# Token tile 0 taken four groups ahead at the ends and heads of layers, and a feed order for each kind of unit

## The chip, the cores and the metric
One core of one Trainium2 chip runs the whole kernel. The metric is the device time of one execution in microseconds; the kernel before is given by the median of 3 runs. Engines: PE is TensorE (matrix products), PEld its weight load, DVE VectorE, ACT ScalarE, POOL GpSimd, SP the engine whose queue issues most DMAs. "L172" is line 172 of the kernel before.

## The reference, cut to what matters
Two layers over 256 tokens of width 2048, batch 1, all in fp32. Each layer is a mixer and a feed-forward net (FFN), each followed by a residual addition and a LayerNorm. The mixer of layer 0 (here mixer 0) is a gated MLP beside a pooling; that of layer 1 (mixer 1) is a gated linear recurrence over 16 heads.

```python
for l in range(2):
    if l % 2 == 0:
        h = x @ ev_w_in[e]                              # 2048 x 3072
        ...
        mix = concatenate([ya, yb]) @ ev_w_out[e]       # 2048 x 2048
    else:
        q, f_logit, inp, g = split(x @ od_w_in[o], 4)   # 2048 x 8192
        y = rms_norm(hgrn2(q, f_logit, inp, lb_all[l]), od_norm_g[o])
        mix = (y * sigmoid(g)) @ od_w_out[o]            # 2048 x 2048
    x = layer_norm(ALPHA * x + mix, ln1_g[l], ln1_b[l])
    x = layer_norm(ALPHA * x + conv_ffn(x, ...), ln2_g[l], ln2_b[l])

def conv_ffn(x, w_up, conv_w, conv_b, w_down):
    h = x @ w_up                                        # 2048 x 11264
    ...                                                 # causal convolution of width 3
    a, v = split(hc, 2)
    return (silu(a) * v) @ w_down                       # 5632 x 2048
```

## The kernel before
**Tiles.** The 256 tokens are two token tiles, t = 0 and 1, of 128 (`x_t[t]`). Weights come as tiles of 512 inputs by 512 outputs, 1 MB each. An fp32 product is made from three products of rounded numbers: a weight w is split into a high half wh (ACT, L172) and a low half wl (DVE, L175; for the feeds in `on_pool` POOL, in four pieces), and an activation likewise; wh·xh, wl·xh and wh·xl are added up in PSUM. So one weight tile and one token tile are 12 matmuls of 512 columns: four slices of 128 inputs, three products each.

**Weights.** `Weights` is a planner that is filled before the kernel is written out: `std`, `quad` and `chain` append feeds, in the order in which the weights will be used, and loads. There are two kinds of loads. Kind 0 uses a ring of three raw tiles (`BUFS`); kind 1 uses the tiles q0 to q3 (an FFN) or qa and qb (mixer 1) of the pool `raw[1]`, one buffer each. `room` lets a load of kind 1 pass only when its phase is `open`; `W.open += 1` stands at the beginning of each FFN and of mixer 1. `take` hands out the next weight; ahead of that it issues all loads for which there is room (kind 1 first) and makes the halves of the two weights that follow. The halves lie in the pool `hl`, three buffers of wh and of wl. All loads are issued on SP's queue; in `quad` and `chain`, sums of weights are made by accumulating DMAs, which POOL issues (L77, L105).

**Layers.** `chunk` makes 512 outputs of both token tiles from four weights; with `head` it takes three weights ahead and runs them for token tile 0, then for token tile 1, then the fourth weight for both, so that token tile 0 can begin while token tile 1 of x is still being normed. After a layer's first chunk `combine` makes the sums of x for the Strassen units. `strassen` makes 2 x 2 blocks (two token tiles, two chunks) from seven products of 12 matmuls (P1 to P7), and four plain groups of 24 ("s"); "o" in its order is a place for one step of the down projection (`down`), 24 matmuls, if there is one. `UNIT_R` is the order for mixer 1, where the order of feeds made by `chain` must be the same one. In a chain P7, P6 and P4 use the tile a in turn: behind P7's cast a load is added to it for P6, behind P6's cast another for P4. Mixer 1 has four head groups `hg` of two units each; group 0 has no down steps (its first unit is two plain chunks), groups 1 and 2 have two in each unit, group 3 one.

**Later work.** Work on vectors is put off by `later(n, fn)` and called by `tick`; 12 matmuls of a unit tick 0.5. In `heads4`, `queries`, `scores`, `outputs` and `transpose_split` of a token tile follow one another in this way; `outputs(t)` makes o, and its transposes on PE make YT, the input of the down steps in the next group.

**The end of a layer.** `last_down` runs the last four down steps (c = 0 to 3) of FFN 0, mixer 1 and FFN 1; mixer 0 ends with `out_proj`. It runs c = 0 for both token tiles, then c = 1 to 3 for token tile 0, then `norm(0)`, then c = 1 to 3 for token tile 1, then `norm(1)`. `after` adds the product to x (L561) and takes statistics (L588); `norm` makes moments (L492, L485, a power on POOL L488), and then for each quarter of x two steps on DVE (L498, L499) and `transpose_split`: four transposes on PE (L480) into a PSUM tile of the tag aux, and its high and low halves on ACT (L270) and DVE (L271). The tag aux has four buffers, the banks acc another four; the products of token tile 1, c = 1 to 3, go to aux:

```python
        def out_bank(t, c):
            if t == 0 or c == 0:
                b = banks.pop(0)
                banks.append(b)
                return acc.tile([P, 512], F32, name="ps", tag=b)
            return aux.tile([P, 512], F32, name="pd", tag="aux")
```

The framework puts the instructions of each engine in a fixed order before run time, by its own estimate of when each is ready, and by the order of the code where several are.

## Time and profile before

| | us |
|---|---|
| median of 3 runs | 2228.1 (2226.89 to 2231.41) |
| the profiled execution | 2226.97 |
| its span in the trace | 2225.3 |
| PE busy | 2164.7 (97%) |
| DVE busy | 1769.9 (80%) |
| ACT busy | 1234.0 (55%) |
| POOL busy | 128.9 (6%) |
| mean granted clock of PE | 0.988 of full |

Busy time of PE includes moments in which matmuls run at the lower clock, and an engine's share is a mean over stages. What PE waits for, and how many matmuls it gets through in a stretch, are read from the views below.

### The profile page before, as it was taken

The page shows a single profiled execution, that of the slowest core. Times are in us where ns is not written, and L with a number is a line of the kernel's source. Part 1 is how long each engine was busy: PE and PEld are TensorE (multiplying, and loading weights), DVE is VectorE, ACT ScalarE, POOL GpSimd, SP SyncE. Part 2 cuts the span into 40 slices and gives each one's busy share as a digit, 9 for nine tenths or more (in the row PEclk, how much of TensorE's full clock was granted, in tenths as well). Part 3 has the DMA queues.
Part 4 walks back from the last instruction along what each step waited for, and adds up shares of the span by engine and source line. Part 5 has one row for each costly group of instructions (what it writes and reads, how often), then busy time and mean ns, then how long its engine had stood idle before and what let it go on. Part 6 is the DMA issues. An engine that isn't in the chain of part 4 may idle for free. (4 is left out here: it accounts for less than half of the span.)

```text
span 2225.3 us, 24817 instructions
## 1 busy us (share of the span) xinstructions
PE 2164.7 (97%) x9887; PEld 1787.4 (80%) x9887; DVE 1769.9 (80%) x1706; ACT 1234.0 (55%) x1153; POOL 128.9 (6%) x140
## 2 busy tenths in 40 slices
PE   9999999999999999979999999989999999999997
PEld 7888788888888888868788888768888888888885
DVE  5545888888888888877677877778888888888888
ACT  5443365555555555536475757536556555555552
POOL 1000200000000000020000101030000000000000
PEclk9999999999999999989999999999999999999999
DMA  8647456767767667546788687755677666777742
GB/s 320 265 160 287 147 184 222 241 228 245 231 219 221 219 226 241 194 146 204 208 246 256 218 257 225 226 185 178 232 241 233 224 221 215 224 243 248 243 153 114
DMA packets 71795, 489.00 MB, mean 220 GB/s; under 512 B 8464, under 2 KB 9120, under 8 KB 13952
## 3 DMA queue, kind: packets, MB, share of 16 engines
q1 hardware_dynamic: 60656, 411.56, 49.6%
q0 software_dynamic: 11024, 75.86, 17.0%
q8 instruction: 77, 1.26, 0.2%
q14 instruction: 38, 0.31, 0.0%
HBM read 443.34 MB, written 2.11 MB: 200 GB/s over the span
## 5 line engine op out<-in xcount | busy, mean ns | idle before, releaser
L175 DVE TENSOR_TENSOR wl<-w,wh 128x2048 fp32r<-128x2048 f32 (+1 forms) x471 | 1051.8, 2236 | 346.8 <-ACT wh L172 345.1
L172 ACT ACTIVATE wh<-w 128x2048 fp32r<-128x2048 f32 (+1 forms) x495 | 894.7, 1813 | 637.2 <-PE pd L553 271.1
L399 PE MATMUL ps<-wh,xh 128*128 128x512 f32 x1188 | 470.4, 396 | 5.2 <-ACT wh L172 5.2
L399 PE MATMUL ps<-wl,xh 128*128 128x512 f32 x1188 | 464.7, 391 | 3.4 <-DVE wl L175 3.4
L399 PE MATMUL ps<-wh,xl 128*128 128x512 f32 x1188 | 464.2, 391 | 0.0
L553 PE MATMUL pd<-wh,yh 128*128 128x512 f32 x760 | 296.9, 391 | 0.0
L553 PE MATMUL pd<-wl,yh 128*128 128x512 f32 x760 | 296.2, 390 | 0.0
L553 PE MATMUL pd<-wh,yl 128*128 128x512 f32 x760 | 295.9, 390 | 0.0
L399 PEld LDWEIGHTS ps<-wh,xh 128*128 128x128 f32 x1188 | 224.1, 189 | 51.4 <-ACT wh L172 6.5
L399 PEld LDWEIGHTS ps<-wl,xh 128*128 128x128 f32 x1188 | 224.3, 189 | 49.5 <-DVE wl L175 5.0
L399 PEld LDWEIGHTS ps<-wh,xl 128*128 128x128 f32 x1188 | 224.0, 189 | 47.2
L399 PE MATMUL ps<-wh,sh 128*128 128x512 f32 x432 | 168.7, 390 | 1.2 <-ACT u L411 1.2
L399 PE MATMUL ps<-wl,sh 128*128 128x512 f32 x432 | 168.2, 389 | 0.0
L399 PE MATMUL ps<-wh,sl 128*128 128x512 f32 x432 | 168.1, 389 | 0.0
L553 PEld LDWEIGHTS pd<-wh,yl 128*128 128x128 f32 x760 | 142.9, 188 | 30.1 <-DVE yl L271 0.4
L553 PEld LDWEIGHTS pd<-wh,yh 128*128 128x128 f32 x760 | 143.1, 188 | 29.6
L553 PEld LDWEIGHTS pd<-wl,yh 128*128 128x128 f32 x760 | 143.0, 188 | 29.6
L332 PE MATMUL ps<-wl,xh 128*128 128x512 f32 x384 | 152.5, 398 | 2.4 <-POOL wl L175 2.3
L332 PE MATMUL ps<-wh,xh 128*128 128x512 f32 x384 | 153.1, 400 | 1.6 <-ACT wh L172 1.6
L332 PE MATMUL ps<-wh,xl 128*128 128x512 f32 x384 | 151.2, 394 | 0.0
L771 DVE SCALAR_TENSOR_TENSOR hc<-ph,cw,hc 128x254 f32<-128x254 f32 (+1 forms) x352 | 145.6, 475 | 1.0 <-ACT hc L768 1.0
L768 ACT ACTIVATE hc<-ph,cw 128x256 f32<-128x256 f32 x176 | 89.3, 557 | 64.9 <-DVE hc L771 61.3
(227 smaller groups left out, 2181.5 us busy)
## 6 DMA issues: line engine op xcount, KB each, us to landing
w<-in_w_up SPq DMA_DIRECT2D x176, 1024.0 KB, 4.9
w<-in_w_down SPq DMA_DIRECT2D x88, 1024.0 KB, 4.9
w<-in_w_od_in SPq DMA_DIRECT2D x64, 1024.0 KB, 6.3
w<-w POOLq DMA_DIRECT2D x40, 1024.0 KB, 8.0
w<-in_w_od_in POOLq DMA_DIRECT2D x21, 1024.0 KB, 9.0
w<-in_w_ev_in SPq DMA_DIRECT2D x20, 1024.0 KB, 5.6
w<-in_w_ev_out SPq DMA_DIRECT2D x16, 1024.0 KB, 4.8
w<-in_w_od_out SPq DMA_DIRECT2D x16, 1024.0 KB, 6.4
```

Of the source, the lines that this page charges most:

```text
L172: self.nc.scalar.activation(h[:, sl], w[:, sl], AF.Copy)
L175: eng.tensor_tensor(out=l[:, sl], in0=w[:, sl], in1=h[:, sl].bitcast(F32), op=ALU.subtract)
L332: T.matmul(ps[t], s[:, k, ts], m[:, k], start=(gi == 0 and k == 0 and i == 0), stop=(gi == n - 1 and k == 3 and i == 2))
L399: T.matmul(bank_, x[:, k, ts], m[:, k], start=(id(bank_) not in started), stop=(k == 3 and i == 2), skip_group_check=True)
L553: T.matmul(ps, x[:, k, t * P:(t + 1) * P], m[:, k], start=(k == 0 and i == 0), stop=(k == 3 and i == 2))
L768: A.activation(ob, pt[:, k], AF.Identity, scale=cw[:, 2, blk:blk + 1], bias=cw[:, 3, blk:blk + 1])
L771: V.scalar_tensor_tensor(out=ob[:, s:S], in0=pt[:, k, 0:S - s], scalar=cw[:, w, blk:blk + 1], in1=ob[:, s:S], op0=ALU.mult, op1=ALU.add)
```

## The change
Five things change.
1. `last_down` gives all products the banks acc. It runs the last `n_skew` groups (4 in the FFNs, 3 in mixer 1) for token tile 0, then the same for token tile 1. The norm of token tile 0 is cut into quarters, one behind each product of token tile 1 (with `n_skew=3` two behind the first).
2. `chunk` with `head` runs all four groups for token tile 0, then all four for token tile 1, and calls `after(t)` right behind each. It no longer ticks.
3. The fourth weight that is then held needs halves beyond the three buffers of `hl`. `extra` puts them into two quad tiles: the fourth feed of each FFN and of mixer 1, and the first feed of the last down steps of each FFN. To leave those tiles free, `W.open += 1` moves behind the first chunk of a layer, and so do the quad loads.
4. `UNIT_R` becomes three orders, by the number of down steps in the unit (0, 1 or 2; the last is the order before).
5. `outputs(t)` comes 1 tick (0.5 in group 3) behind the later of `scores(t)` and `after_i(t)`, where it came 1 + t ticks (half of it in group 3) behind `after_i`; the transposes of o come 1.5 ticks behind the outputs, where it was 1 (0.5 in group 3 as before).

```diff
--- before.py
+++ after.py
@@ -25,7 +25,9 @@
 ALPHA = float(np.float32(4.0 ** 0.25))
 WIN = (2, 4, 8, 16)
 SKEW = 3
-UNIT_R = ("P1", "s", "P7", "s", "P3", "P2", "P6", "o", "P5", "o", "P4", "s", "s")
+UNIT_R = (("P1", "P7", "s", "P3", "s", "P6", "P2", "P5", "s", "P4", "s"),
+          ("P1", "s", "P7", "s", "P3", "P2", "P6", "o", "P5", "s", "P4", "s"),
+          ("P1", "s", "P7", "s", "P3", "P2", "P6", "o", "P5", "o", "P4", "s", "s"))
 UNIT = ("P1", "s", "P2", "s", "P3", "o", "P7", "o", "P6", "o", "P5", "o", "P4", "s", "s")
 BUFS = 3
 EDGE = 244
@@ -46,6 +48,8 @@
         self.ring = {}
         self.done = {}
         self.on_pool = set()
+
+        self.extra = {}
 
 
     def _load(self, ap, tag):
@@ -99,6 +103,7 @@
 
         nc = self.nc
         a, b = self._load(aps[3], "qa"), self._load(aps[2], "qb")
+        unit = UNIT_R[len(others)]
         rest, others = iter(rest), iter(others)
 
         def add(ap):
@@ -112,7 +117,7 @@
         products = {"P7": (a, (), None, lambda: add(aps[0])), "P3": (b,), "P6": (a, (b,), None, t1),
                     "P5": (b,), "P4": (a,)}
         plain = {"P1": aps[0], "P2": aps[1]}
-        for f in UNIT_R:
+        for f in unit:
             if f in products:
                 self._feed(*products[f])
             else:
@@ -157,8 +162,9 @@
     def cast(self, pieces=1, between=None):
         i = self.n_cast
         w = self.feeds[i]["r"]["tile"]
-        h = self.hl.tile([P, 4, 512], F32R, name=f"wh{i}", tag="wh")
-        l = self.hl.tile([P, 4, 512], F32R, name=f"wl{i}", tag="wl")
+        pool, tags = (self.raw[1], self.extra[i]) if i in self.extra else (self.hl, ("wh", "wl"))
+        h = pool.tile([P, 4, 512], F32R, name=f"wh{i}", tag=tags[0])
+        l = pool.tile([P, 4, 512], F32R, name=f"wl{i}", tag=tags[1])
         if i in self.on_pool:
             pieces, eng = 4, self.nc.gpsimd
         else:
@@ -219,6 +225,7 @@
 
     def plan_ffn(l):
         W.on_pool |= {len(W.feeds) + i for i in range(2)}
+        W.extra[len(W.feeds) + 3] = ("q1", "q3")
         up, down = a["w_up"][l], a["w_down"][l]
         W.phase += 1
         for p in range(11):
@@ -230,10 +237,12 @@
             W.quad([up[p, 0], up[p, 1], up[11 + p, 1], up[11 + p, 0]],
                    [up[p, 2], up[p, 3], up[11 + p, 2], up[11 + p, 3]], now)
         W.std([down[c, 9] for c in (2, 3)])
+        W.extra[len(W.feeds)] = ("q1", "q3")
         W.std([down[c, 10] for c in range(4)])
 
     plan_ffn(0)
     W.on_pool |= {len(W.feeds) + i for i in range(2)}
+    W.extra[len(W.feeds) + 3] = ("qa", "qb")
     W.phase += 1
     wi, wo = a["w_od_in"], a["w_od_out"]
     for hg in range(4):
@@ -334,12 +343,16 @@
                              stop=(gi == n - 1 and k == 3 and i == 2))
 
         order = list(range(n))
-        first = order[:SKEW] if head else []
+        first = order if head else []
         last = order[-SKEW:] if tail else []
         ws = [W.take() for _ in first]
         for t in range(2):
             for gi, w in zip(first, ws):
                 mm(gi, w, t)
+            if first:
+                after(t, ps[t])
+        if first:
+            return
         for gi in order[len(first):n - len(last)]:
             if gi == n - 1:
                 tick(9)
@@ -570,47 +583,53 @@
             tick(0.5)
             add_x(t, c, ps, scale)
 
-    def last_down(get, g_ap, b_ap, final):
+    def last_down(get, g_ap, b_ap, final, n_skew=4):
 
         gt, bt = load_gb(g_ap, b_ap)
         sts = [small.tile([P, 4, 6], F32, name=f"st{t}") for t in range(2)]
         new = [new_T("x", g) for g in range(4)] if not final else None
-        pool_of = {}
-
-        def out_bank(t, c):
-            if t == 0 or c == 0:
-                b = banks.pop(0)
-                banks.append(b)
-                return acc.tile([P, 512], F32, name="ps", tag=b)
-            return aux.tile([P, 512], F32, name="pd", tag="aux")
+        def out_bank():
+            b = banks.pop(0)
+            banks.append(b)
+            return acc.tile([P, 512], F32, name="ps", tag=b)
 
         def after(t, c, ps):
             V.bn_stats(sts[t][:, c], add_x(t, c, ps, False))
 
-        def norm(t):
-            mean, rs = moments(sts[t])
-            for q in range(4):
-                qs = slice(q * 512, (q + 1) * 512)
-                normalize(x_t[t][:, qs], x_t[t][:, qs], mean, rs, gt[:, qs], bt[:, qs])
-                if final:
-                    nc.sync.dma_start(out[t * P:(t + 1) * P, qs], x_t[t][:, qs])
-                else:
-                    transpose_split(new[q], x_t[t][:, qs], t)
+        def norm(t, q, mean, rs):
+            qs = slice(q * 512, (q + 1) * 512)
+            normalize(x_t[t][:, qs], x_t[t][:, qs], mean, rs, gt[:, qs], bt[:, qs])
+            if final:
+                nc.sync.dma_start(out[t * P:(t + 1) * P, qs], x_t[t][:, qs])
+            else:
+                transpose_split(new[q], x_t[t][:, qs], t)
 
         tick(9)
         Ts = get()
-        w = W.take()
-        for t in range(2):
-            ps = out_bank(t, 0)
-            product(ps, w, Ts, t)
-            after(t, 0, ps)
-        ws = [W.take() for _ in range(3)]
-        for t in range(2):
-            for c, w in zip((1, 2, 3), ws):
-                ps = out_bank(t, c)
+        for c in range(4 - n_skew):
+            w = W.take()
+            for t in range(2):
+                ps = out_bank()
                 product(ps, w, Ts, t)
                 after(t, c, ps)
-            norm(t)
+        skewed = range(4 - n_skew, 4)
+        ws = [W.take() for _ in skewed]
+        for c, w in zip(skewed, ws):
+            ps = out_bank()
+            product(ps, w, Ts, 0)
+            after(0, c, ps)
+        mean, rs = moments(sts[0])
+        todo = list(range(4))
+        for c, w in zip(skewed, ws):
+            ps = out_bank()
+            product(ps, w, Ts, 1)
+
+            while len(todo) > 3 - c:
+                norm(0, todo.pop(0), mean, rs)
+            after(1, c, ps)
+        mean, rs = moments(sts[1])
+        for q in range(4):
+            norm(1, q, mean, rs)
         return new
 
 
@@ -739,7 +758,6 @@
         with ExitStack() as pools:
             wk = pools.enter_context(tc.tile_pool(name=f"workf{l}", bufs=1))
             raw[1] = pools.enter_context(tc.tile_pool(name=f"rawq{l}", bufs=1))
-            W.open += 1
             cwp = pools.enter_context(tc.tile_pool(name=f"cw{l}", bufs=1))
             cw = cwp.tile([P, 4, 2 * NF], F32, name="cw")
             G.dma_start(cw, a["conv"][l].rearrange("p (j n) -> p j n", j=4))
@@ -793,6 +811,7 @@
             done = ready(0)
             chunk(XT, 4, conv(0, done), head=True)
             tmp = [wk.tile([P, 4, S], F32, name="cmb", tag="hc", bufs=2) for _ in range(2)]
+            W.open += 1
             XS = combine(XT, *(v[:, :, ts] for v in tmp for ts in (np.s_[0:P], np.s_[P:S])))
             chunk(XT, 4, conv(1, done))
             for p in range(1, 11):
@@ -811,7 +830,6 @@
         yp = pools.enter_context(tc.tile_pool(name="ymix1", bufs=1))
         raw[1] = pools.enter_context(tc.tile_pool(name="rawq", bufs=1))
         wk = pools.enter_context(tc.tile_pool(name="work1", bufs=1))
-        W.open += 1
         YT = []
         tri_r = wk.tile([P, P], F32R, name="tri_r")
         A.activation(tri_r, tri, AF.Copy)
@@ -843,6 +861,7 @@
         def heads4(hg):
             qs = slice(hg * 512, (hg + 1) * 512)
             eb, kd, ke, kx, qd, qx, vv, o_s, st, gg = {}, {}, {}, {}, {}, {}, {}, {}, {}, {}
+            parts = [0, 0]
 
             def tile_f(name="f"):
                 return wk.tile([P, 512], F32, name=name, tag="ta", bufs=2)
@@ -927,12 +946,19 @@
                 for k in range(4):
                     T.matmul(px[:, k], kx[t][:, k], qd[t][:, k, hi], start=True, stop=True)
                 A.activation(att[t][lo, :, hi], px, AF.Copy)
+                both(t)
 
             def after_i(t, v):
                 vv[t] = v
                 if t == 0:
                     later(0.5, state)
-                later((1 + t) / (1 if hg < 3 else 2), lambda: outputs(t))
+                both(t)
+
+            def both(t):
+
+                parts[t] += 1
+                if parts[t] == 2:
+                    later(1 if hg < 3 else 0.5, lambda: outputs(t))
 
             def state():
                 pu = aux.tile([P, 4, P], F32, name="pu", tag="aux")
@@ -968,7 +994,7 @@
                     YT.append(tuple(y))
                 if t == 1 and hg < 3:
                     bounds(hg + 1)
-                later(1 if hg < 3 else 0.5, lambda: transpose_split(YT[hg], o, t))
+                later(1.5 if hg < 3 else 0.5, lambda: transpose_split(YT[hg], o, t))
 
             def after_g(t, ps, g):
                 A.activation(g, ps, AF.Sigmoid)
@@ -984,12 +1010,13 @@
                     for t in range(2):
                         (done1, done2)[c](t, tiles[t])
 
-                strassen(XT, XS[0], tile_of, done, downs, UNIT_R)
+                strassen(XT, XS[0], tile_of, done, downs, UNIT_R[len(downs)])
 
             n_out = 2 if hg < 3 else 1
             downs = [lambda c=c: down(c, YT[hg - 1], hg == 1) for c in range(4)] if hg else []
             if hg == 0:
                 chunk(XT, 4, lambda t, ps: after_f(t, ps, tile_f()), head=True)
+                W.open += 1
                 tmp = [wk.tile([P, 4, P], F32, name="cmb", tag=g, bufs=2) for g in ("eb", "eb", "kd", "kd")]
                 XS.append(combine(XT, *tmp))
                 chunk(XT, 4, lambda t, ps: after_g(t, ps, tile_g()))
@@ -1003,7 +1030,7 @@
             rest = heads4(hg)
         for fn in rest:
             fn()
-        XT = last_down(lambda: YT[3], a["ln1_g"][1], a["ln1_b"][1], False)
+        XT = last_down(lambda: YT[3], a["ln1_g"][1], a["ln1_b"][1], False, n_skew=3)
         del raw[1]
 
     ffn(1, XT, True)
```

## Rows read from the trace of the kernel before

**Rows 1.** The page, section 1: busy time, share of span, instructions of each engine.

```profile
PE 2164.7 (97%) x9887; PEld 1787.4 (80%) x9887; DVE 1769.9 (80%) x1706; ACT 1234.0 (55%) x1153; POOL 128.9 (6%) x140
```

**Rows 2.** Waits of PE: who waited for whom: us in total, times, longest us.

```profile
PE pt L480 <- DVE x L499: 20.8, 8, 4.3
PE pt L480 <- DVE o L960: 5.8, 4, 1.5
PE ps L399 <- ACT wh L172: 5.2, 3, 3.8
...
PE ps L399 <- DVE wl L175: 3.4, 4, 1.8
```

**Rows 3.** PE by stretches: length, PE busy (matmuls), granted clock, DMA share, GB/s.

```profile
238.00:256.00 18.00, 13.40 (x59) 0.91 0.24 74
962.00:1000.00 38.00, 27.71 (x115) 0.82 0.43 144
1063.00:1079.00 16.00, 11.23 (x36) 0.79 0.72 238
1417.50:1427.00 9.50, 6.75 (x22) 0.82 0.80 294
1470.00:1503.00 33.00, 24.44 (x100) 0.84 0.54 166
```

**Rows 4.** The same stretches, transposes of x (tile pt) alone.

```profile
962.00:1000.00 38.00, 6.94 (x32) 0.82 0.43 144
1470.00:1503.00 33.00, 4.62 (x24) 0.84 0.54 166
```

**Rows 5.** Timeline of PE, FFN 0 to mixer 1: start, us, instruction [idle before <-releaser].

```profile
967.27 1.41 PE L480 MATMUL pt<-cst,x 128*128 128x128 f32 x8 [4.07 <-DVE x L499]
...
990.54 1.08 PE L480 MATMUL pt<-cst,x 128*128 128x128 f32 x4 [4.29 <-DVE x L499]
```

**Rows 6.** Timeline of PE, head group 0, transposes of o for token tile 1.

```profile
1116.16 0.63 PE L480 MATMUL pt<-cst,o 128*128 128x128 f32 x4 [1.44 <-DVE o L960]
```

**Rows 7.** Timelines of DVE and POOL, norm of token tile 0 (FFN 0, mixer 0).

```profile
965.06 1.41 DVE L498 SCALAR_TENSOR_TENSOR x<-x,mv,g 128x512 f32<-128x512 f32 x2
...
243.43 3.47 DVE L498 SCALAR_TENSOR_TENSOR x<-x,mv,g 128x512 f32<-128x512 f32 x2
...
241.36 12.49 POOL L175 TENSOR_TENSOR wl<-w,wh 128x512 fp32r<-128x512 f32 x8 [0.44 <-ACT wh L172]
```

**Rows 8.** Timelines of POOL, ACT and PE, mixer 1's first unit.

```profile
1059.22 0.86 POOL L105 DMA_DIRECT2D w<-in_w_od_in  x1 [15.01 <-DVE wl L175]
...
1068.27 3.71 ACT L172 ACTIVATE wh<-w 128x2048 fp32r<-128x2048 f32 x2 [4.88 <-DMA w<-in_w_od_in]
...
1070.23 0.50 PE L399 MATMUL ps<-wh,xh 128*128 128x512 f32 x1 [3.77 <-ACT wh L172]
```

**Rows 9.** Timelines of POOL and ACT, mixer 1's last unit.

```profile
1407.03 0.85 POOL L105 DMA_DIRECT2D w<-in_w_od_in  x1 [15.62 <-DVE wl L175]
...
1416.71 3.71 ACT L172 ACTIVATE wh<-w 128x2048 fp32r<-128x2048 f32 x2 [5.64 <-DMA w<-in_w_od_in]
```

**Rows 10.** Timelines of PE and DVE at the end of the kernel.

```profile
2210.71 0.39 PE L553 MATMUL pd<-wl,yh 128*128 128x512 f32 x1
...
2212.98 0.39 PE L553 MATMUL pd<-wh,yl 128*128 128x512 f32 x1
...
2212.36 1.28 DVE L561 TENSOR_TENSOR x<-x,pd 128x512 f32<-128x512 f32 x2
...
2215.46 0.69 DVE L588 BATCH_NORM_STATS2 st<-x 128x6 f32<-128x512 f32 x1
...
2220.53 1.41 DVE L499 SCALAR_TENSOR_TENSOR x<-x,rs,b 128x512 f32<-128x512 f32 x2
```

**Rows 11.** The page, section 6 (KB, us to landing); a stretch with all engines, DMA last.

```profile
w<-in_w_up SPq DMA_DIRECT2D x176, 1024.0 KB, 4.9
...
1460.00:1470.00 10.00, 10.00 (x46) 8.29 (x45) 7.73 (x8) 3.84 (x2) 0.68 (x1) 1.00 1.00 406
```

## The prediction, made before the change was run

> **What bounds the kernel now.** Read section 1 of the page first: TensorE (PE) is busy for 97% of the span, VectorE (DVE) for 80%, ScalarE (ACT) for 55%, GpSimd (POOL) for 6% [rows 1]. So the end is set by PE, and only two things can shorten the kernel: fewer PE instructions (the change removes none) or fewer moments in which PE stands still or runs slowly. Read PE's waits next. Almost all of them are of a few kinds [rows 2]: transposes of the normalized x wait for DVE (20.8 us in 8 waits), transposes of the attention output o wait for DVE (5.8 us in 4), and products in the Strassen units wait for the high and low halves of a weight (5.2 and 3.4 us).
>
> Then read PE by stretches, because a wait is only part of the loss: after one, the granted clock is low for a while. Eleven 512-column matmuls in a row start from 2210.71 to 2212.98, one each 0.227 us [rows 10]; four transposes take 0.63 us, about 0.12 us each [rows 6]. What a stretch loses is its length less 0.227 us per product matmul and 0.12 per transpose:
> - FFN 0 to mixer 1, 962 to 1000: 115 matmuls, 32 of them transposes [rows 3, 4]. 38 - 83 x 0.227 - 32 x 0.12 = **15.3 us** lost. Its two largest idle pieces are 4.07 and 4.29 us [rows 5], and the mean clock is 0.82 [rows 3], that is part of it at the lower of the two levels, 1.2 GHz.
> - Mixer 1 to FFN 1, 1470 to 1503: 100, of them 24 transposes [rows 3, 4]. 33 - 76 x 0.227 - 24 x 0.12 = **12.9 us**.
> - Mixer 0 to FFN 0, 238 to 256: 59, of them 16 transposes (token tile 0's four quarters). 18 - 43 x 0.227 - 16 x 0.12 = **6.3 us** [rows 3].
> - The first Strassen unit of mixer 1, 1063 to 1079: 36, four of them short. 16 - 32 x 0.227 - 4 x 0.12 = **8.3 us** [rows 3].
> - The last unit of mixer 1, 1417.5 to 1427: 9.5 - 22 x 0.227 = **4.5 us** [rows 3].
> - Three waits of 1.44 us and a little more for o, in head groups 0 to 2: **4.3 us** [rows 6].
>
> **The layer ends.** Before, the last products run c0 for both token tiles, then c1 to c3 for token tile 0, then its norm, then c1 to c3 for token tile 1. These last write PSUM tiles of the tag aux, whose four buffers the four transposed quarters have just taken. So no product of token tile 1 can be issued ahead of the transposes, and PE stands while DVE makes the moments and the quarters. The change gives all products the acc banks, and puts each quarter behind a product of token tile 1: 12 matmuls, 2.7 us, lie between two quarters. PE then has 36 matmuls (mixer 1) or 48 (FFN 0) beside the norm.
>
> The other end case has this shape already: at the end of mixer 0 the norm of token tile 0 runs beside 36 matmuls. It still loses 6.3 us, and the reason moves along with the change. POOL makes the low halves of the next layer's first two weights (8 pieces, 12.49 us) as soon as ACT has a free weight buffer, and during that a pair of DVE norm steps takes 3.47 us (two pairs do) where it takes 1.41 alone [rows 7]. Before, at the end of FFN 0, the norm of token tile 0 was over before POOL began. After, a buffer comes free when the second product of token tile 1 is done, so POOL begins some 5 us, two products, before the last one ends and meets the last quarters of the norm. So I don't take the loss to zero but to the measured 6.3 us: FFN 0 to mixer 1 gains 15.3 - 6.3 = **9.0 us** (bounds: 2, if all quarters are met, and 15.3). At mixer 1 there are only three products, 8.2 us, for 16 norm and split steps and three additions with statistics, so I add 1.5 us to what stays: 12.9 - 7.8 = **5.1 us** (0 to 12.9).
>
> The Trainium skill states the reason as a rule (SBUF — State Buffer, section Who interferes with whom): a DVE instruction with two inputs in SBUF and a GpSimd instruction that reads SBUF lock each other out for a whole instruction. The trace agrees: 3.47 against 1.41 us for two [rows 7]. The rule speaks against the change, which brings more such pairs together; taken for every quarter it is the first rival.
>
> **The heads.** Token tile 0 now runs all four groups (48 matmuls, 10.9 us) before token tile 1, where it ran three, so the norm of token tile 1 has 2.7 us more cover. What DVE is late by at the end of the products comes back here: eight norm steps of 0.66 us and four additions with statistics of 1.33 [rows 10] are 10.6 us, and with the splits more than the 10.9 of four products. I count nothing for that, since the head's 48 matmuls cover it. The fourth weight must be there 8.2 us into the head. Its load waits for the first weight's raw tile, which POOL holds; then it takes 4.9 us [rows 11], and its halves are two more steps on ACT and on a busy DVE. I charge **1 us** for all heads together (bounds: 1 gained, 6 lost). On ACT the two sigmoids of mixer 1's first chunk part, so the activation tables change twice more; ACT has 45% to spare [rows 1].
>
> The quad loads (four of 1 MB for each FFN, two for mixer 1, on SP's queue, with the accumulating DMA that POOL issues behind each set) wait for the head's fourth weight to be used up, as it lies in two of their buffers. They are moved past the loads of the second chunk's weights, which the head's own takes have issued, and past POOL's low halves, done by then. Their first user comes one chunk later, 96 matmuls or 21.8 us. Four MB at the 406 GB/s that the queues reached [rows 11] are 10.4 us, and an accumulating load behind takes 9 us (below). Mixer 1: 5.2 + 9 + 2 for the casts is 16 of 24.5 us (P7 now comes right behind P1). Cost nothing; if the cover is gone, the rival on the other side.
>
> **The units with few down steps.** In mixer 1's first unit POOL issues the last accumulating load of the chain at 1059.22, when P6's halves are made; ACT makes the halves of P4 at 1068.27, after 9 us, and PE, having only P5 in between, waits 3.77 us and starts P4 at 1070.23, then runs at a mean clock of 0.79 [rows 3, 8]. The unit has no down steps to fill the places marked o. The new order sets P2 and a plain group (2.7 and 5.4 us) between P6 and P4, beside P5: 8.2 us more, against a wait of 3.8. P7 to P6 gets 2.7 us more too, so the load before has no new trouble. 8.3 us go but for 0.5 that I leave: **7.8 us** (4 to 8.3). In head group 3 the same wait (issue 1407.03, halves 1416.71 [rows 9]) has a plain group more in front of it, 5.4 us against 2.8 of waits: 4.5 us. But that group no longer lies behind P4. The queries start from P4, and the outputs of head group 3 so move next to the last products, with 2.7 us less behind them. I take 2 us off: **2.5 us** (1 lost to 4.5).
>
> **The outputs.** In head groups 0 to 2 the transposes of o come 1.5 instead of 1 tick behind the outputs, half a tick being 12 matmuls or 2.7 us, and token tile 1's outputs come half a tick sooner. A wait of 1.44 us is then covered by matmuls: **4.3 us** (1 to 4.3). What waits behind is the split of y, used half a tick later at the earliest.
>
> **The tail.** PE's last matmul starts at 2212.98; DVE then is in arrears with token tile 0's norm, adds two results at 2212.36 and ends at 2221.94 [rows 10]. With token tile 0 done one product sooner DVE has 10.9 us for 5.3 of norm and 4.0 of three additions, so it waits for PE: 2213.4 + 1.4 (an addition of 0.64 and statistics of 0.69 [rows 10]) + 0.5 until the norm (now 2221.94 - 5.28 - 2216.15) + 8 x 0.66 = 2220.6, with 0.1 of gaps **1.2 us** less (0 to 1.2).
>
> **Sum.** 9.0 + 5.1 + 7.8 + 2.5 + 4.3 + 1.2 - 1.0 = 28.9 us. The profiled execution took 2226.97 us, its span 2225.3; the median of the runs is 1.1 above it. 2226.97 - 28.9 = 2198.1, so for a median **2199 us**.
>
> **The rivals.**
> 1. *POOL's low halves meet the whole norm.* Eight pieces hold up eight DVE steps by 1.0 us each ((3.47 - 1.41) / 2), 8.2 us at each of two ends, where I allow for about half. For it: in mixer 0 at least four of eight steps were met (the two pairs of 3.47 us [rows 7]); against: in FFN 0 three quarters should be over before POOL starts. 2199 + 2 x 4 = 2207.
> 2. *PE's order doesn't change where it counts*: the transposes still stand ahead of products that could cover them, as the order was fixed before run time. The ends give nothing: 2199 + 14 = 2213. Against it: the end of mixer 0, where 13 matmuls do stand between quarters.
> 3. *The units wait for bytes and not for order.* The DMA share in both stretches is 0.72 and 0.82 [rows 3], not 1. Then 7.8 and 2.5 don't come: 2209.
> 4. *All stalls go.* The ends keep 2 us each and not 6.3 and 7.8: 2199 - 10, and no charge at the heads: 2188.
> 5. *Slower: SP stands at the quad loads.* SP's queue is served in order; the first quad load waits for the head's last matmul. Were the second chunk's four weight loads placed behind it, PE would wait for 4 MB of quads (10.4 us), a load (4.9) and a cast (2) in each FFN, less what is buffered: about 16, in mixer 1 about 10. 2199 + 42 = 2241. It decides from about three of the four loads on. Against it: the code issues them first.
>
> **How the numbers follow.** Forecast 0.55, rivals 0.17, 0.07, 0.05, 0.10 and 0.06. The terms' bounds do not all meet at one end; half of them going badly costs 15 us, half going well gives 13. Range 2184 to 2216: it takes in rivals 1 to 3 and most of 4, and leaves out rival 5 and the tails, some 0.18. A measurement tells 0.2% (4.5 us) from no change: faster 0.90, within it 0.04 (rivals 2 and 3 together), slower 0.06.
>
> **What the profile after would show.** PE's waits for x fall from 20.8 us to below 10; the stretch from FFN 0 to mixer 1 loses 6 us and not 15; POOL's eight pieces lie beside DVE norm steps of 1.7 us; the wait for P4 is gone in both units; no transposes of o wait in groups 0 to 2; the new waits to look for are of products at a head on the fourth weight, and of transposes in the last products. I am wrong if the second chunk of a layer waits for loads, or if the ends lose as much as now.

## The result, and the profile after

The changed kernel took **2203.1 us** (median of four runs, 2196.8 to 2204.2) beside 2227.6 for the kernel before in the same runs: a ratio of 0.988, 95% interval 0.986 to 0.990. That is 24.5 us less, inside the predicted range and 4 us above the predicted 2199. A second set of runs gave 2199.9 (2196.0 to 2208.8), 0.986 [0.984, 0.989]. The single runs of this kernel lie up to 13 us apart; why is one of the findings below.

The profiled execution took 2203.0 us with a span of 2201.2, against 2227.0 and 2225.3 before. Section 1 of the page after, with the same columns as [rows 1]:

```profile
PE 2157.1 (98%) x9887; PEld 1779.9 (81%) x9887; DVE 1767.4 (80%) x1706; ACT 1230.3 (56%) x1150; POOL 125.8 (6%) x140
```

The same 9887 PE instructions: nothing was taken away, PE only stands or runs slowly for less time. The waits of PE after (who waited for whom: us in total, times, longest us):

```profile
PE pt L493 <- DVE x L512: 10.8, 8, 2.7
PE pt L493 <- DVE o L986: 4.2, 3, 1.4
PE pa L943 <- DVE eb L929: 3.3, 1, 3.3
PE pd L566 <- DVE x L574: 3.2, 2, 1.7
PE ps L412 <- DVE wl L181: 2.2, 3, 1.1
PE pb L485 <- DVE fl L280: 2.1, 1, 2.1
PE ps L341 <- ACT wh L178: 1.6, 2, 1.4
...
PE pt L493 <- DVE ss L500: 1.0, 1, 1.0
```

Against [rows 2]: the wait for x is halved (20.8 to 10.8); the waits of the Strassen units for a high half (5.2) are off the list; the wait for o is still there (5.8 in four, now 4.2 in three, and a fourth listed under ss); pa for eb and pd for x are new, and pb for fl has grown. In the same list before, last products waited for yh where pd now waits for x, and pb waited for 0.5 us:

```profile
PE ps L553 <- ACT yh L270: 5.0, 2, 2.5
...
PE pb L472 <- DVE fl L271: 0.5, 1, 0.5
```

PE by stretches (length, PE busy and matmuls, granted clock, DMA share, GB/s):

```profile
238.00:256.00 18.00, 13.40 (x65) 1.00 0.23 79
950.00:990.00 40.00, 35.86 (x165) 0.96 0.34 128
1063.00:1079.00 16.00, 15.30 (x84) 1.00 0.74 209
1079.00:1095.00 16.00, 13.35 (x73) 0.89 0.52 132
1376.00:1386.00 10.00, 7.39 (x30) 0.83 0.52 97
1412.00:1427.00 15.00, 15.00 (x76) 1.00 0.74 290
...
1455.00:1490.00 35.00, 32.78 (x145) 0.95 0.45 165
```

The transposes of x in two of the ends, in the same columns:

```profile
950.00:990.00 40.00, 5.42 (x32) 0.96 0.34 128
...
1455.00:1490.00 35.00, 4.76 (x28) 0.95 0.45 165
```

By the prediction's reckoning (length less 0.227 us per product matmul and 0.12 per transpose) FFN 0 to mixer 1 loses 40 - 133 x 0.227 - 32 x 0.12 = **6.0 us**, where it lost 15.3 [rows 3, 4]. From mixer 1 to FFN 1, 145 matmuls from 1455 to 1490 with 28 transposes among them lose **5.1 us**, where it was 12.9. The first unit's P4, which waited 3.77 us and left the clock at 0.79 [rows 3, 8], now comes near 1058 without a wait, and the clock from 1063 to 1079 is 1.00. But behind it, from 1079 to 1095, the clock is 0.89, and from 1376 to 1386 it is 0.83: these are the waits for eb and fl.

To compare kernels I add up, over all matmuls, the time between two starts beyond what the form takes at full clock, and call it PE's excess. The full-clock time of a form is its usual step, 0.227 us for a product matmul; taken by form or by line, it moves the totals by up to a microsecond. It is 90.8 us in the kernel before and 68.1 after: 22.7 us less. The tail from the last matmul to the end of the span fell from 12.3 to 10.9. Together 24.1, which is the difference of the two spans.

### The profile page after: what moved, and what is told of

Its sections match the earlier page's. It is cut to its first block, busy times and chain, and to the rows that moved or that the text cites. A ratio compares the mean times of both kernels' runs of the same rounds, so it can differ in the third digit from the quotient of the medians.

```text
span 2201.2 us, 24814 instructions
## 1 busy us (share of the span) xinstructions
PE 2157.1 (98%) x9887; PEld 1779.9 (81%) x9887; DVE 1767.4 (80%) x1706; ACT 1230.3 (56%) x1150; POOL 125.8 (6%) x140
## 5 line engine op out<-in xcount | busy, mean ns | idle before, releaser
L566 PE MATMUL pd<-wh,yh 128*128 128x512 f32 x736 | 287.2, 390 | 3.2 <-DVE x L574 3.2
L566 PE MATMUL pd<-wl,yh 128*128 128x512 f32 x736 | 286.5, 389 | 0.4 <-DVE wl L181 0.4
L566 PE MATMUL pd<-wh,yl 128*128 128x512 f32 x736 | 286.4, 390 | 0.5 <-DVE yl L280 0.4
L566 PEld LDWEIGHTS pd<-wh,yh 128*128 128x128 f32 x736 | 138.2, 188 | 32.5 <-DVE x L574 4.0
L566 PEld LDWEIGHTS pd<-wh,yl 128*128 128x128 f32 x736 | 138.1, 188 | 30.3 <-DVE yl L280 1.6
L566 PEld LDWEIGHTS pd<-wl,yh 128*128 128x128 f32 x736 | 138.2, 188 | 29.3 <-DVE wl L181 0.8
```

The lines of the kernel that those rows point to most:

```text
L566: T.matmul(ps, x[:, k, t * P:(t + 1) * P], m[:, k], start=(k == 0 and i == 0), stop=(k == 3 and i == 2))
```

## The experiments

Each run was timed beside the kernel before on its own chip, so ratios are compared; 0.001 of ratio is 2.2 us.

**The last products alone.** The kernel before with the new `last_down` and the two buffers for the fourth last weight, nothing else.

```
+        W.extra[len(W.feeds)] = ("q1", "q3")
         W.std([down[c, 10] for c in range(4)])
...
-    def last_down(get, g_ap, b_ap, final):
+    def last_down(get, g_ap, b_ap, final, n_skew=4):
...
```

> The kernel before with the new last products alone (all products in the acc banks, a quarter of the norm behind each product of token tile 1, and the two buffers for the fourth last weight); old heads, unit orders and outputs. Theory: these are the whole gain, 9.0, 5.1 and 1.2 us by the prediction and some 21 us as the stretches of the changed kernel show them, so 2206 to 2212 us. Rival: they need the head of four groups behind them, and without it give half: 2215 to 2220 us.

Measured 2206.3 us (2203.3 to 2208.3), 0.9895 [0.9879, 0.9910]: nearly the whole gain, as the first theory has it. Excess before and here: FFN 0 to mixer 1 (925 to 1025 us) 20.7 to 12.5, mixer 1 to FFN 1 (1425 to 1500) 16.9 to 8.8, the last products of FFN 1 (2150 to 2200) 5.9 to 2.6; the tail gives 1.4.

**The PSUM buffers alone.** The kernel before, products and norm written in the old order.

```
-            if t == 0 or c == 0:
-                b = banks.pop(0)
...
-            return aux.tile([P, 512], F32, name="pd", tag="aux")
+            b = banks.pop(0)
+            banks.append(b)
+            return acc.tile([P, 512], F32, name="ps", tag=b)
```

> The kernel before with one thing changed: all last products write PSUM tiles of the acc banks; the order in which they and the norm are written in the source stays (all of token tile 0, its norm, then token tile 1). Theory, the prediction's account: only the four aux buffers held the products of token tile 1 behind the transposes, and with other buffers they are placed ahead of them and beside them: the ends gain 10 us or more, 2207 to 2217 us. Rival: the order in the source decides, and the transposes still stand ahead of the products: 2225 to 2230 us.

Measured 2214.0 us (2213.1 to 2216.2), 0.9936 [0.9924, 0.9949]: 14 us from a change of tags. In the program built from it eight transposes of token tile 0 stand in the middle of the second of the three products of token tile 1 that used to follow them, and the next eight among the matmuls of the third, though the source still has all of them first. So the buffers were what held PE, as the prediction said. The remaining 8 to 9 us of the last products (by the medians, by the ratios) come with the new order. PE's timeline (start, us, [idle before <-releaser]) of this kernel ahead of and in FFN 0's last products:

```profile
947.90 0.50 PE L553 MATMUL ps<-wh,yh 128*128 128x512 f32 x1 [2.52 <-ACT yh L270]
969.15 0.63 PE L480 MATMUL pt<-cst,x 128*128 128x128 f32 x4 [1.06 <-DVE x L499]
975.36 0.66 PE L480 MATMUL pt<-cst,x 128*128 128x128 f32 x4 [2.61 <-DVE x L499]
```

The first line is a wait that I had not priced. It stands ahead of the last products of either FFN. With the new order it is a wait of 1.5 to 1.7 us, of a down product for x; what in the order shortens it was not taken apart.

**The heads undone.** Three groups for token tile 0, the quads opened where they were.

```
-        first = order if head else []
+        first = order[:SKEW] if head else []
...
-            if first:
-                after(t, ps[t])
-        if first:
-            return
```

> The changed kernel with heads of three groups and the old quad loads; the fourth weight's two buffers go with it. Theory, the prediction's account: the fourth group covers nothing that is short, and the head costs at most 1 us: 2201 to 2204 us. Rival: with three groups the norm of token tile 1, which still waits for POOL's low halves, is 2.7 us short of cover at each of three heads, and the clock falls behind the wait: 2208 to 2214 us, with longer waits of transposes of x.

Measured 2211.0 us (2210.1 to 2213.2), 0.9918 [0.9904, 0.9933] where the changed kernel has 0.9881 and 0.9863: the rival is right. The largest piece is at the head of FFN 1 (PE's timeline):

```profile
1475.36 1.12 PE L487 MATMUL pt<-cst,x 128*128 128x128 f32 x4 [4.37 <-DVE x L506]
```

The changed kernel has no such wait there: its longest at this end are 0.93 and 1.11 us. From 1425 to 1500 us the excess is 14.7 against 11.4, and from 1000 to 1025 it is 2.2 against 0.2; the rest of the 8 us is not placed. What the heads are worth depends on the units, as the section on the last products and the first unit shows.

**The unit orders undone.** All seven units in the old order.

```
-UNIT_R = (("P1", "P7", "s", "P3", "s", "P6", "P2", "P5", "s", "P4", "s"),
-          ("P1", "s", "P7", "s", "P3", "P2", "P6", "o", "P5", "s", "P4", "s"),
-          ("P1", "s", "P7", "s", "P3", "P2", "P6", "o", "P5", "o", "P4", "s", "s"))
+UNIT_R = (("P1", "s", "P7", "s", "P3", "P2", "P6", "o", "P5", "o", "P4", "s", "s"),) * 3
```

> The changed kernel with the old order in all seven units of mixer 1. Theory: the new orders only moved the wait of the chain, from P4 of a unit to P7 of the next unit, because P4's halves are made one plain group later and the two loads of the next unit start behind them. Then the waits of the first unit (8 us) and of the last one (5 us) come back, and the waits at 1081 us (6 us), 1380 us (5 us) and about 2 us near 1443 go: 2203 us, between 2200 and 2206. Rival, the prediction's account: the new orders are worth 7.8 and 2.5 us net, so the kernel takes 2213 us.

Measured 2204.6 us (2202.4 to 2207.5), 0.9889 [0.9873, 0.9905]: part 4, for which I had 10.3 us, is worth 2 to 5 by the medians (2203.1 and 2199.9 with it), and the intervals overlap. PE's timeline here, in the first unit and in the last:

```profile
1056.92 0.51 PE L410 MATMUL ps<-wh,xh 128*128 128x512 f32 x1 [3.72 <-ACT wh L176]
...
1406.64 0.50 PE L410 MATMUL ps<-wh,xh 128*128 128x512 f32 x1 [1.60 <-ACT wh L176]
1408.97 0.50 PE L410 MATMUL ps<-wl,xh 128*128 128x512 f32 x1 [1.82 <-DVE wl L179]
```

The old waits are back, and the new ones are gone. In the excess, in slices of 25 us: from 1050 on 7.0 and 2.6 here, 0.4 and 7.1 in the changed kernel; 1375 and 1400: 0.2 and 5.8 here, 5.0 and 0.0 there. How the wait moved is seen in the changed kernel's timelines of POOL, ACT, DVE and PE, where one unit passes into the next:

```profile
1063.53 0.84 POOL L110 DMA_DIRECT2D w<-in_w_od_in  x1 [21.12 <-DVE u L453]
...
1076.75 1.92 ACT L178 ACTIVATE wh<-w 128x2048 fp32r<-128x2048 f32 x1 [9.58 <-DMA w<-in_w_od_in]
...
1078.70 2.29 DVE L181 TENSOR_TENSOR wl<-w,wh 128x2048 fp32r<-128x2048 f32 x1 [10.99 <-ACT wh L178]
1080.91 0.68 DVE L929 TENSOR_TENSOR eb<-pq,eb 128x512 f32<-128x512 f32 x1
...
1081.65 2.07 PE L943 MATMUL pa<-eb,kd 128*128 128x128 f32 x8 [3.35 <-DVE eb L929]
```

P4's cast frees the raw tile for the next unit's load and the accumulating load behind it. With P4 one plain group later, the accumulating load is issued at 1063.53 and P7's halves can't be made before 1076.75. ACT and DVE work in order: DVE stands 11 us at this one low half, and eb, which needs none of it, is behind it; the scores on PE wait for eb.

**The same kernel once more.** The changed kernel, unchanged, on another chip.

> The changed kernel itself, on the chip of the three runs beside it, so that they can be compared with it directly. Both theories: 2203 us, between 2200 and 2206, with waits of about 3.5 us at 1081 us and 2.3 us at 1380 us again.

2199.9 us, but 2196.0 to 2208.8, and the profiled execution, a span of 2194.2 us, has neither of the two waits. There the load took less:

```profile
1063.11 0.84 POOL L110 DMA_DIRECT2D w<-in_w_od_in  x1 [19.04 <-DMA w<-in_w_od_in]
...
1072.36 1.92 ACT L178 ACTIVATE wh<-w 128x2048 fp32r<-128x2048 f32 x1 [3.20 <-DMA w<-in_w_od_in]
```

9.3 us from issue to cast here and 13.2 in the other execution, for the same megabyte. So with the new orders the wait comes in some executions and not in others; their excess, 68.1 and 61.1, differs by 7.0, mostly in these two places. Three more kernels here keep these orders and let the scores follow the same way (the heads undone, one tick, the low halves on DVE); the profiled execution of each has the wait for eb (3.0, 3.3 and 2.3 us). The old orders pay in the one profiled (67.6).

**The chain spread evenly.** The unit without down steps gets one plain group between P6 and P4 and keeps two behind P4; the first unit of head group 3 has the old order, its second the new.

```
-UNIT_R = (("P1", "P7", "s", "P3", "s", "P6", "P2", "P5", "s", "P4", "s"),
+UNIT_R = (("P1", "P7", "s", "P3", "P2", "P6", "s", "P5", "P4", "s", "s"),
...
+def unit_r(hg, u):
+    return UNIT_R[0 if hg == 0 else 1 if (hg, u) == (3, 1) else 2]
```

> The changed kernel with the chain spread evenly: the unit with no down steps gets one plain group between P6 and P4 and keeps two behind P4, the first unit of head group 3 gets the old order, the last unit keeps the new one. Theory: a chain product needs some 8 us of matmuls between P6 and P4 and some 17 us between P4 and the next P7, and the new orders gave the first by taking from the second. Then the waits at 1081 us (5.9 us without the wait for o) and at 1380 us (5.0 us) go and none comes back: 2192 us, between 2190 and 2197. Rival: the loads themselves are too slow in these stretches, and the wait only turns up at the next product: 2201 to 2205 us.

Measured 2198.1 us (2195.9 to 2199.6), 0.9866 [0.9851, 0.9881]. Both waits are gone in the profiled execution, and the runs spread over 3.7 us, where those of the changed kernel spread over 7 and 13. But the wait for the first unit's P4, gone in the changed kernel, is partly back; the slice from 1050 has an excess of 3.8. PE's timeline, then POOL's (the load that is added to the tile for P4) and ACT's:

```profile
1052.19 0.50 PE L417 MATMUL ps<-wh,xh 128*128 128x512 f32 x1 [0.52 <-ACT wh L183]
1054.51 0.50 PE L417 MATMUL ps<-wl,xh 128*128 128x512 f32 x1 [1.82 <-DVE wl L186]
...
1040.22 0.85 POOL L115 DMA_DIRECT2D w<-in_w_od_in  x1 [14.44 <-DVE wl L186]
...
1050.22 1.91 ACT L183 ACTIVATE wh<-w 128x2048 fp32r<-128x2048 f32 x1 [6.07 <-DMA w<-in_w_od_in]
```

From the issue to the cast are 10.0 us, and two halves have to be made. The changed kernel has 48 matmuls between P6 and P4 there, 10.9 us, and this one 36, 8.2 us: the "some 8 us" that I took for enough are not. That is a part of the 6 us by which it came out above the 2192 that I expected.

**The last products and the first unit.** The first experiment's kernel with that order in the first unit alone.

```
-UNIT_R = ("P1", "s", "P7", "s", "P3", "P2", "P6", "o", "P5", "o", "P4", "s", "s")
+UNIT_R = (("P1", "P7", "s", "P3", "P2", "P6", "s", "P5", "P4", "s", "s"),) + (
+          ("P1", "s", "P7", "s", "P3", "P2", "P6", "o", "P5", "o", "P4", "s", "s"),) * 2
```

> The kernel before with the new last products and one new unit order: in the first unit of mixer 1 a plain group between P6 and P4, and two behind P4; old heads, old outputs, old order in the other six units. Theory: the first unit gives back 4 to 8 us here without a wait at 1081 us, and the heads are worth nothing by themselves: 2206 less 5, so 2199 to 2203 us. Rival: the heads are worth 8 us with any new order of the units, as they were beside the change's own orders (2211 without them): 2206 to 2211 us.

Measured 2200.2 us (2197.9 to 2205.0), 0.9862 [0.9843, 0.9882], on the chip that gave the changed kernel 2199.9. So two edits reach the median of the whole change there, and with old heads. The 8 us that the heads were worth beside the change's own orders are not seen beside the old ones. Three runs on one chip show the same: old heads and old orders (the last products alone, which have the old outputs too) take 2206.3 us, new heads and old orders (the unit orders undone) 2204.6, old heads and new orders (the heads undone) 2211.0. So beside the old orders the heads, with part 5, are worth 1.7 us, within the noise, and with old heads the new orders cost time. The place is the end of mixer 1: from 1425 to 1500 us the excess is 8.8, 8.3 and 14.7 in these three, and 11.4 with both new. The last unit's new order costs some 3 us there with heads of four groups and 6 with three, and the fourth group at FFN 1's head pays back what that order takes. That the later outputs of head group 3 are the reason fits, but was not tried alone.

**The outputs undone, and the transposes one tick behind.** First both edits of part 5:

```
-                later(1 if hg < 3 else 0.5, lambda: outputs(t))
+                later((1 + t) / (1 if hg < 3 else 2), lambda: outputs(t))
...
-                later(1.5 if hg < 3 else 0.5, lambda: transpose_split(YT[hg], o, t))
+                later(1 if hg < 3 else 0.5, lambda: transpose_split(YT[hg], o, t))
```

> The changed kernel with the outputs and the transposes of o at their old ticks. Theory: the transposes of o still wait 1.2 to 1.6 us in the changed kernel, because a low half of 2.3 us stands ahead of the last step of o on DVE's queue wherever the transposes are put, so undoing this part changes nothing: 2203 us, between 2201 and 2205, with four waits of 1.4 to 1.6 us again. Rival, the prediction's account: the half tick is worth 4.3 us, so 2207 us.

2199.0 us (2194.4 to 2208.1). With the new orders the scores of head group 3 come after its outputs here, which then take the scores of the head group before, so this kernel computes something else and leaves out a wait; its profiled execution has one of 10.1 us for att instead. It decides nothing. The second undoes the half tick alone:

```
-                later(1.5 if hg < 3 else 0.5, lambda: transpose_split(YT[hg], o, t))
+                later(1 if hg < 3 else 0.5, lambda: transpose_split(YT[hg], o, t))
```

> The changed kernel with the transposes of o at 1 tick behind the outputs and not 1.5; the outputs stay where the change put them. Theory: a low half stands ahead of the last step of o on DVE's queue at either place, so four waits of 1.2 to 1.6 us stay four waits of 1.2 to 1.6 us: 2203 us, between 2201 and 2205. Rival, the prediction's account: the half tick of 2.7 us covers the wait, so without it the kernel takes 2207 us.

Measured 2202.5 us (2197.4 to 2206.4), 0.9882 [0.9865, 0.9899]: no change. **The transposes 2.5 ticks behind**, on the evenly spread units:

```
-                later(1.5 if hg < 3 else 0.5, lambda: transpose_split(YT[hg], o, t))
+                later(2.5 if hg < 3 else 0.5, lambda: transpose_split(YT[hg], o, t))
```

> The evenly spread units, with the transposes of o written 2.5 ticks behind the outputs and not 1.5: 24 more matmuls, 5.4 us, between. Theory: the last step of o is placed on DVE's queue in front of wherever the transposes are, with a low half of 2.3 us ahead of it, so waits of some 1.4 us stay with 60 matmuls between outputs and transposes too: 2196 to 2200 us, as without it. Rival, the prediction's account with another size: half a tick was too little and a tick and a half is enough, the three waits in groups 0 to 2 go: 2194 us.

2196.8 us (2195.9 to 2199.3), 0.9846 [0.9831, 0.9860]. Here my theory fell in its mechanism: the waits in groups 0 to 2 do go. PE's timeline in head group 1, the transposes of token tile 1 and what waits next:

```profile
1217.56 0.60 PE L498 MATMUL pt<-cst,o 128*128 128x128 f32 x4
1224.69 0.50 PE L571 MATMUL pd<-wh,yl 128*128 128x512 f32 x1 [0.24 <-DVE yl L285]
```

The wait of 1.43 us becomes one of 0.24 for yl. Yet the excess of the whole profiled execution is 61.1 us, as it was without the edit (61.0): places of 1.0 to 1.4 us elsewhere made up for it, two of them at the end of mixer 0, where the edit changes nothing. Its time is not told apart from that of the evenly spread units; it ran on another chip.

**The low halves on DVE.** The changed kernel without POOL's pieces.

```
-        W.on_pool |= {len(W.feeds) + i for i in range(2)}
+        W.on_pool |= {len(W.feeds) + i for i in range(0)}
```

The line stands twice, for the FFNs and for mixer 1, and is changed in both places.

> The changed kernel with the low halves of the first two weights of a layer made by DVE (2.3 us each) and not by POOL in eight pieces. Theory, the prediction's account of what the ends still lose: POOL's pieces stretch the norm steps beside them from 0.7 to 1.7 us, and POOL's queue holds the pow of token tile 1's norm behind them; without them the three ends lose some 3 us less each, 2193 to 2198 us. Rival: DVE is itself the last at the ends, and 4.6 us more on it at each cost more than the pieces do: 2206 to 2214 us.

Measured 2200.9 us (2198.7 to 2206.4), 0.9880 [0.9864, 0.9896]: neither. Excess at the three ends, changed kernel and here: mixer 0 to FFN 0 5.6 and 2.8, FFN 0 to mixer 1 9.5 and 11.2, mixer 1 to FFN 1 11.4 and 13.5. At the end of mixer 0, where DVE has time, the pieces are the loss. At the end of mixer 1 DVE has three additions with statistics besides, and a head product waits 2.1 us for a low half that DVE now makes. At the end of FFN 0 the waits for x come to 3.6 us in one here and to 4.1 in three in the changed kernel; what is more is a wait of 1.6 us at 1026.56, in the first Strassen unit, for a high half that ACT makes behind two sigmoids. Why ACT is late there was not taken apart.

**Both kernels beaten.** The evenly spread units, and POOL's pieces left out at FFN 0's head alone:

```
-        W.on_pool |= {len(W.feeds) + i for i in range(2)}
+        W.on_pool |= {len(W.feeds) + i for i in range(2 if l else 0)}
```

> The evenly spread units, and at the head of FFN 0 alone the low halves of the first two weights made by DVE and not by POOL. Theory: at the end of mixer 0 the pieces of POOL are what makes the quarters late; with all low halves on DVE that stretch lost 2.8 us where it loses 5.6 (the other two ends lost 2 us more), so 2.8 us less than the evenly spread units alone: 2195 us, between 2192 and 2198. Rival: DVE is as late with 4.6 us more to do, and the loss only moves behind the head: 2197 to 2200 us.

Measured **2193.0 us** (2191.7 to 2197.6), 0.9830 [0.9815, 0.9846], beside 0.9863 [0.9839, 0.9888] for the changed kernel on the same chip: by the medians 7 us better than the change and 39 better than before. Against the change the intervals just overlap (by 0.0007), against its first set of runs they do not. Beside the evenly spread units the excess from 225 to 275 us falls by 2.8 us, as the theory had it. Its waits for x fell from 11.0 us in 8, in the evenly spread units, to:

```profile
PE pt L498 <- DVE x L517: 6.1, 5, 1.9
```

## Why the prediction was right, and where it was not

The time and the sign came out. The terms of the ends and the tail were sound, those of the units, the outputs and the heads were not. Where two numbers stand, they are of the two profiled executions of the changed kernel.

- **FFN 0 to mixer 1, 9.0 us:** 15.3 to 6.0, so 9.3. Right in the gain: the products cover the quarters. And POOL's pieces meet the last quarters, as told. DVE's and POOL's timelines after:

```profile
959.89 0.75 DVE L511 SCALAR_TENSOR_TENSOR x<-x,mv,g 128x512 f32<-128x512 f32 x1
...
964.26 1.66 DVE L511 SCALAR_TENSOR_TENSOR x<-x,mv,g 128x512 f32<-128x512 f32 x1
...
968.74 1.83 DVE L511 SCALAR_TENSOR_TENSOR x<-x,mv,g 128x512 f32<-128x512 f32 x1
...
964.08 11.93 POOL L181 TENSOR_TENSOR wl<-w,wh 128x512 fp32r<-128x512 f32 x8 [3.68 <-issue]
...
977.51 0.58 POOL L501 TENSOR_TENSOR rs<-rs,mhalf 128x1 f32<-128x1 f32 x1
...
974.93 2.08 DVE L840 CAST msk<-cst 128x128 uint8<-128x128 f32 x1
976.01 1.01 DVE L498 TENSOR_SCALAR rs<-mv 128x1 f32<-128x1 f32 x1
```

  A step of 0.75 us takes 1.66 and 1.83 beside the pieces, in agreement with the Trainium skill's rule (SBUF — State Buffer, section Who interferes with whom) on DVE steps with two inputs in SBUF; additions of a product, which have one input in PSUM, keep their 0.68 there. Four steps were met, by 2.9 us in all, and at the end of mixer 1 six, by 3.9, not eight by 8.2, so rival 1 did not come. What I missed are the last lines: token tile 1's statistics end at 974.2, but a cast of a mask (2.08 us, others of its kind 0.2 to 0.7) and the moments' last step (1.01 us, for token tile 0 0.15) hold rs until 977.02, and POOL's queue holds the pow for 0.5 us more. That what stays is 6.0, next to the 6.3 taken over from mixer 0, is in part luck: without the pieces most of it goes at the end of mixer 0 but not here (the low halves on DVE).
- **Mixer 1 to FFN 1, 5.1 us:** 12.9 to 5.1, so 7.8 by the prediction's stretches. But some 2.5 us now stand just ahead of the stretch, where the last unit's new order has brought the outputs next to the last products: a product waits 0.7 us for y, and the clock is low behind it; the 2 us taken off in the units were meant for this. From 1425 to 1500 us, with these, the excess falls from 16.9 to 11.4, so 5.5. The 1.5 us that I had added for the shorter cover of three products were not needed, even with heads of three groups (the last products alone, 16.9 to 8.8).
- **The first unit and head group 3, 7.8 and 2.5 us:** wrong step. The waits for P4 went, as costed. But "the queries start from P4" was followed for head group 3 only, and the loads of the next unit, which start from P4 as well, not at all. From 1050 to 1125 us the excess fell from 11.7 to 10.7 or 4.3, from 1350 to 1425 from 7.6 to 5.2 or 3.0. Rival 3 (bytes, not order) has a part in it: during the load behind P4 the DMA queues are full (below), and how long it takes decides.
- **The outputs, 4.3 us:** next to nothing. The three waits were 4.4 us together and are 3.8 or 2.8. "A wait of 1.44 us is then covered by matmuls" counted the matmuls, not the chain. In groups 1 and 2 there were 33 product matmuls in the 11.4 us between the starts of the outputs and the transposes of token tile 1, and there are 42 in 13.4 us after, and the last gap between two starts is 1.8 us as before. The change also brought the two outputs closer, from 6.35 to 3.6 us, and on DVE a low half of 2.3 us came to lie between the last two steps of o. With 60 matmuls the wait goes. DVE's timeline after, in head group 1:

```profile
1216.05 1.14 DVE L984 SCALAR_TENSOR_TENSOR o<-o,ss,ng 128x128 f32<-128x128 f32 x4 [0.90 <-POOL ss L501]
1217.10 2.29 DVE L181 TENSOR_TENSOR wl<-w,wh 128x2048 fp32r<-128x2048 f32 x1
1219.30 0.69 DVE L986 TENSOR_TENSOR o<-o,c 128x512 f32<-128x512 f32 x1
```
- **The heads, -1.0 us:** wrong sign. That the head's 48 matmuls cover what DVE is late by was true. Beside the new orders 36 do not (8 us by the medians), beside the old ones they nearly do (1.7 us). The activation tables are not changed twice more: ACT has 32 table loads before and 29 after.
- **The tail, 1.2 us:** 1.4. DVE did wait for PE's last product, as told.
- **Not in the sum:** the wait ahead of FFN 1's last products, 2.5 us and the low clock behind it, which fell from 5.9 to 2.7.
- **The rivals:** 2 and 5 are excluded by the traces (quarters stand between products; no second chunk waits for the quads). 4 did not come: by the stretches the ends still lose 6.0 and 5.1 us, not 2 each.

So 28.9 was predicted and 24.0 measured. By the excess, which adds up where the stretches do not, the ends gave some 16.5 for 14.1, FFN 1's last products 3.2 that no term held, the tail 1.4, and the units and the outputs some 3.4 of 14.6; all other slices differ by less than 1 us together. That the total came within 5 us is in part luck: of the 11 us that did not come, more than half was made up for by gains that the sum did not have.

## What to carry to other kernels

When a product of a chain is moved later, follow what starts from it, first of all the load into the buffer that it frees; then look for independent work behind the new late step in the in-order queues of the engines. A wait is not covered by putting as many matmuls in front as it is long: count from the start of the chain that it ends, since the chain's own steps move too. And before rewriting an order by hand, look at which buffers forbid the scheduler the order: one tag gave 14 of 25 us here.

## What the hardware showed that was not expected

An accumulating load of 1 MB, issued at the same point of the same kernel, took 9.3 us from issue to its cast in one execution and 13.2 in another. In both, SP issued three plain loads of 1 MB within 5 us of it, and the DMA queues were full at a low rate (busy time of PE, PEld, DVE, ACT and POOL, granted clock, DMA share, GB/s; first the execution with 13.2 us):

```profile
1064.00:1069.00 5.00, 5.00 (x26) 4.12 (x25) 3.40 (x4) 0.63 (x2) 0.38 (x1) 1.00 0.99 257
1069.00:1074.00 5.00, 5.00 (x31) 4.33 (x30) 0.00 (x0) 0.00 (x0) 0.00 (x0) 1.00 1.04 280
```

```profile
1064.00:1069.00 5.00, 5.00 (x25) 4.16 (x25) 4.69 (x6) 2.11 (x3) 0.00 (x0) 1.00 1.01 210
1069.00:1074.00 5.00, 5.00 (x29) 4.27 (x28) 0.69 (x1) 1.80 (x2) 0.00 (x0) 1.00 1.00 356
```

A share of 1.0 at 210 to 280 GB/s, and in the fourth stretch at 356, where plain loads reached 406 [rows 11]: in these stretches, with an accumulating load under way for all or most of the time, the queues were full without moving as much. A rate alone would have shown room where there was none. What made the one load longer stays open.
